# A hybrid decoder layer on one core: filler projections moved ahead of a triangular solve, a last transpose behind a filler, and an output projection begun feature tile by feature tile

## The chip, the cores and the metric

The kernel runs on one core of one Trainium2 chip. The core has a matrix engine (TensorE, PE in the profile), a vector engine (VectorE, DVE), a scalar engine (ScalarE, ACT), a general engine (GpSimd, POOL) and SyncE (SP), which here issues the DMA transfers. Each engine works through its own row of instructions in order, and waits on semaphores for the others. The metric is the device time of one execution in microseconds (us), the median of the runs.

## The reference

One layer on `x` of 1024 positions by 1024 features, all in float32:

```python
h = rmsnorm(x, g_mix)
proj = h @ w_in                                   # 64 tiles of 128 output features and 16 more
y_fox = forgetting_attention(fq, fk, fv, ...)     # 8 heads of 64
y_sc = sb * causal_dwconv(sc * sv, sc_conv_w)
o_dn = gated_delta_rule(l2norm(dq), l2norm(dk_), dv_, g, beta)   # 4 heads of 128
y_dn = rmsnorm(o_dn, dn_norm_gain) * silu(z)
merged = jnp.sum(jnp.einsum('bsnc,ncd->bsnd', ys, w_branch) * gates, axis=2)
x = x + merged @ w_o
...
# gated_delta_rule: for each chunk a unit lower triangular system
a_mat = jnp.where(strict, einsum(kb, kc) * decay, 0.0) + jnp.eye(c)
sol = lax.linalg.triangular_solve(a_mat, rhs, left_side=True, lower=True, unit_diagonal=True)
```

After it come an up projection with a convolution and a gate, a down projection and a per-layer embedding, which the change does not touch.

## The kernel before, in words

Activations lie with the features on the partitions, as eight tiles of 128 features by 1024 positions. Each f32 operand is split in a high and a low part (`split`, L129 on ScalarE, L130 on VectorE or POOL), and one 128 x 128 block of weights is three matmuls of 128x512 (`step`, all at L126): high by high, high by low, low by high. `dense` makes an output tile in two halves of 512 positions; a half of a tile over all eight feature tiles is 24 matmuls into one PSUM bank, and then `evac` reads the bank.

The program is a row of stages. `fx` holds the first norm, the attention, and in `f2` the DeltaNet part; `la`/`me` the gates, the short convolution, the three branch products and the output projection; then come the up and the down stage.

**The DeltaNet stage.** `dn_solve` inverts the triangular systems. For each of eight pairs of chunks ("chunk" below) and four heads it loads kc (tile `kc`, 4 buffers) and a row of decays (`gb`, 3 buffers), multiplies kc by itself on TensorE (tiles `sm`), builds A on VectorE, moves the 32 x 32 diagonal blocks together (L728), and inverts all of them at once by a recursion over 31 rows on VectorE (L734, L736). The inverses are transposed back into TT (L739) and into X (L748), and then products on TensorE put blocks of 64 and of 128 together (`to64`, `add64`, `to128`, `add128`), of which the first is X by A1. `dn_prep` loads ks, qc and vc of a chunk and transposes them on TensorE through one bank (tiles `ev`; L796, L800; VectorE reads them at L797 and L801), `dn_state` carries the state from chunk to chunk (products of w and X, vn, S), and `dn_out` makes a chunk's output in the bank `po`, squares it on ScalarE (L854), scales it (L855 to L859), transposes it (L862) and stores it.

**Fillers.** These stages leave TensorE free in places. So 32 output tiles of the first projection that are needed only later lie in `spare["r"]`: each ("r") is a `raw_tile`, that is a weight load (`wr`, 2 buffers), its split into `wo` (5 buffers), 48 matmuls in two banks, and for each bank an evacuation by ScalarE (L503) and a store (L504). `filler` takes such tiles and gives them to the scheduler with the condition that they come after a matmul noted by `mark`:

```python
def filler(kinds, back=LAG):
    for k in kinds:
        if spare.get(k):
            with tc.issue_after(marks[max(0, len(marks) - 1 - back)]):
```

How many stand where is in the table `PLAN`. The final order on each engine is set by a scheduler that simulates the program, so that table and code order steer it, but don't fix it. In `f2` fillers have two PSUM banks, `sm` four, `ev` and `po` one each.

**The output projection** (L1030 to L1041). `mh` holds the merged activations, eight feature tiles split in two halves each. A feature tile is merged when the third branch (b == 2) has been multiplied by its gate (L1019) and added (L1020, on POOL), and then split at L129 and L130. Then `dense` makes one output tile after another over all eight feature tiles, with six PSUM banks; `ev_o` (L1036) adds x.

Of the kernel before, what the change touches and what calls it, by code (L numbers as in the profile page):

```python
# [10 lines left out]
ALU = mybir.AluOpType  # L11
# [19 lines left out]
PLAN = {"start": "krr", "tail": "rr", "solve": "rrrrrrrrrrrrr",  # L31
        "steps": ["rr", "r", "r", "r", "r", "r", "r", "r", "r"],
# [16 lines left out]
def hybrid_block(ctx: ExitStack, tc: tile.TileContext, I, out, dbg=None):  # L49
# [37 lines left out]
    def bank(role):  # L87
        pool, n = homes[role]
        return pool.tile([P, 512], F32, tag=role, name=nm(role), bufs=n)
# [565 lines left out]
    def hs(h):  # L655
        return slice(h * P, h * P + P)
# [53 lines left out]
    def dn_solve():  # L710
# [26 lines left out]
        for b in range(4):  # L737
            p = slice(32 * b, 32 * b + 32)
            V.transpose(out=TT[p, :, p].rearrange("p x c -> p c x"), in_=TL[p].rearrange("p r c -> p c r"))  # L739
        Ac, Tc = ([x[:, 4 * c : 4 * c + 4, :] for c in range(8)] for x in (A, TT))  # L740
# [105 lines left out]
    def dn_out(c, Sst, vn, pd, qe):  # L846
# [13 lines left out]
        pot = bank("po")  # L860
        for h in range(4):
            nc.tensor.transpose(pot[:, hs(h)], o[:, hs(h)], ident)  # L862
        yo = pt("yo", 2)
        S.activation(yo, pot, AF.Copy, scale=col(C_NG))
        Q.dma_start(ydn[:, :, hs(c)], chunk(yo))
# [15 lines left out]
    with phase("fx", psum=dict(mm=MM, ev=1), cv=3, o=4, sg=2, h=1, l=1, y=1,  # L881
# [31 lines left out]
        with phase("f2", psum=dict(sm=SM2, po=1), X=8, et=2):  # L913
            mark()
            with phase("f2s"):
                Xs = dn_solve()
                mark()
                filler(PLAN["solve"], 1)
            with phase("f2t"):
                preps = [dn_prep(0), dn_prep(1)]  # L920
                Ss, vns = [None], []
                for c in range(9):
# [5 lines left out]
                    if c:  # L928
                        dn_out(c - 1, Ss[c - 1], vns[c - 1], *preps[c - 1][3:])
                    if 2 <= c + 1 < 8:  # L930
                        preps.append(dn_prep(c + 1))
                    filler(PLAN["steps"][c], 1)
                filler("r" * len(spare["r"]), 0)

# [9 lines left out]
    with phase("la", psum=dict(mm=6, sm=2), a=16, wq=3):  # L944
        with phase("me", tmp=9, sg=4, yr=4):
# [50 lines left out]
            for b in range(3):  # L996
# [5 lines left out]
                for d2 in range(4):  # L1002
# [9 lines left out]
                    for dt in (2 * d2, 2 * d2 + 1):  # L1012
                        def ev_b(nb, ps, dt=dt):
# [6 lines left out]
                            G.tensor_tensor(out=m, in0=m, in1=t, op=ALU.add)  # L1020
# [9 lines left out]
            x2s = []  # L1030
            for dt in range(8):
                x2 = big()
                Q.dma_start(x2, I["xT"][dt])

                def ev_o(nb, ps):
                    V.tensor_tensor(out=x2[:, NB[nb]], in0=ps, in1=x2[:, NB[nb]], op=ALU.add)  # L1036
                dense(wload(I["wo"][dt]), KT, mh, ev_o)
                summed = sumsq(acc, x2, dt == 0, (V, G))
                Q.dma_start(x2dr[dt], x2)
                x2s.append(x2)  # L1040
# [216 lines left out]
```

## Time and profile before

| | us |
|---|---|
| median of 3 runs | 2005.56 (2003.4 to 2006.41) |
| the profiled execution | 2005.48 |
| its span, first to last instruction | 2003.7 |
| VectorE / ScalarE / POOL busy in it | 1338.9 / 908.0 / 531.3 |
| chain that ended last, by engine: PE / DVE | 17% / 10% |

The profile is that of one execution. The mean granted TensorE clock is 0.992 of full speed. The chain that ended last is followed back only as far as waits lead, and most of the span TensorE simply works one matmul after another, so the chain names little; where TensorE stands idle, and for whom, is read from its waits. In the names of the rows "mm<-xg,wo" is a matmul of activations xg with weights wo into a bank mm; the buffer's number is left out in the trace and is there in the order of instructions.

### The profile page before, as it was taken

How to read it: one execution, taken by the hardware profiler on the slowest of the kernel's cores; microseconds unless marked ns; L12 is line 12 of the kernel's file. 1: busy time of each engine (PE TensorE's matmuls, PEld its weight loads, DVE VectorE, ACT ScalarE, POOL GpSimd, SP SyncE). 2: the span in 40 equal slices, each digit the busy share in tenths (PEclk: the TensorE clock that was granted, in tenths of full speed). 3: DMA queues.
4: the chain of work that ended last, by engine and by line, in shares of the span. 5: the costliest groups of instructions: out<-in, count | busy, mean ns of one | idle time of the engine just before them, and what ended most of it. 6: DMA issues, size and time to landing. Idle time of an engine off the chain costs nothing. (4 is left out here: it accounts for less than half of the span.)

```text
span 2003.7 us, 25407 instructions
## 1 busy us (share of the span) xinstructions
PE 1943.1 (97%) x9281; PEld 1611.3 (80%) x9281; DVE 1338.9 (67%) x2157; ACT 908.0 (45%) x1651; POOL 531.3 (27%) x435
## 2 busy tenths in 40 slices
PE   8999999999997999999999999999999999999998
PEld 6888888888786888878888787778777778888887
DVE  6878788788496203429757438787878788544564
ACT  6576777677321324333423326454444444211351
POOL 1455334434322222100034110333434340000210
PEclk9999999999998999999999999999999999999999
DMA  4221112122521334447853423112222226332132
GB/s 176 70 98 57 59 59 76 62 83 76 150 91 53 100 106 126 122 155 281 302 191 121 174 91 130 53 47 91 75 84 74 84 74 252 115 95 78 49 114 86
DMA packets 102636, 219.40 MB, mean 109 GB/s; under 512 B 9360, under 2 KB 40432, under 8 KB 102512
## 3 DMA queue, kind: packets, MB, share of 16 engines
q1 hardware_dynamic: 102512, 217.79, 32.1%
q8 instruction: 73, 1.20, 0.3%
q14 instruction: 51, 0.42, 0.1%
HBM read 158.98 MB, written 58.77 MB: 109 GB/s over the span
## 5 line engine op out<-in xcount | busy, mean ns | idle before, releaser
L126 PE MATMUL mm<-xg,wo 128*128 128x512 f32 x6128 | 1488.0, 393 | 17.7 <-DVE wo L130 12.2
L126 PEld LDWEIGHTS mm<-xg,wo 128*128 128x128 f32 x6128 | 1141.7, 189 | 260.6 <-DVE wo L130 19.4
L126 PE MATMUL mm<-a,wo 128*128 128x512 f32 x1216 | 306.1, 391 | 3.1 <-ACT a L129 3.1
L126 PEld LDWEIGHTS mm<-a,wo 128*128 128x128 f32 x1216 | 229.8, 189 | 52.2 <-ACT a L129 4.2
L129 ACT ACTIVATE wo<-wr 128x512 fp32r<-128x512 f32 x232 | 144.6, 626 | 267.8 <-PE mm L126 255.1
L130 POOL TENSOR_TENSOR wo<-wr,wo 128x512 fp32r<-128x512 f32 x108 | 149.1, 1383 | 320.0 <-ACT wo L129 312.1
L1159 DVE TENSOR_TENSOR a<-mm,a 128x512 f32<-128x512 f32 x96 | 65.3, 689 | 92.1 <-PE mm L126 92.0
L130 DVE TENSOR_TENSOR wo<-wr,wo 128x512 fp32r<-128x512 f32 x124 | 89.6, 724 | 27.4 <-ACT wo L129 26.8
L280 POOL TENSOR_TENSOR tmp<-tmp,tmp 128x512 f32<-128x512 f32 x21 | 27.8, 1324 | 286.0 <-ACT tmp L278 284.1
L1020 POOL TENSOR_TENSOR a<-a,sg 128x512 f32<-128x512 f32 x32 | 48.1, 1508 | 191.7 <-DVE sg L1019 191.5
L130 DVE TENSOR_TENSOR wo<-wq,wo 128x512 fp32r<-128x512 f32 x68 | 79.2, 1167 | 3.2 <-ACT wo L129 3.2
L503 ACT ACTIVATE o<-mm 128x512 f32<-128x512 f32 x60 | 35.8, 596 | 93.9 <-PE mm L126 62.5
L1072 DVE SCALAR_TENSOR_TENSOR o<-cw,cols,o 128x1024 f32<-128x1024 f32 x44 | 77.8, 1769 | 0.0
L491 DVE SCALAR_TENSOR_TENSOR o<-cv,cols,o 128x512 f32<-128x512 f32 x72 | 69.9, 971 | 10.2 <-ACT o L489 9.2
L129 ACT ACTIVATE wo<-ws 128x512 fp32r<-128x512 f32 x80 | 50.2, 630 | 56.7 <-PE mm L126 54.9
L600 ACT ACTIVATE pp<-pp,small 128x512 f32<-128x512 f32 (+2 forms) x96 | 58.4, 610 | 28.7 <-DVE small L594 28.4
L1104 POOL TENSOR_TENSOR cg<-o,cg 128x1024 f32<-128x1024 f32 x22 | 55.5, 2522 | 39.7 <-ACT cg L1103 39.7
L199 POOL TENSOR_TENSOR ws<-wq 128x512 f32<-128x512 f32 x20 | 29.7, 1487 | 122.7 <-DMA wq<-wup 122.7
L1070 ACT ACTIVATE o<-cw,cols 128x1024 f32<-128x1024 f32 x22 | 25.4, 1156 | 74.8 <-DVE cw L223 74.8
L130 DVE TENSOR_TENSOR pl<-pq,ph 128x512 fp32r<-128x512 f32 (+1 forms) x80 | 49.9, 629 | 13.9 <-ACT ph L129 13.5
L199 POOL TENSOR_TENSOR ws<-wq,wq 128x512 f32<-128x512 f32 x20 | 43.7, 2183 | 56.3 <-DVE wo L130 52.3
L199 DVE TENSOR_TENSOR ws<-ws,wq 128x512 f32<-128x512 f32 x20 | 14.9, 745 | 64.2 <-POOL ws L199 64.2
(290 smaller groups left out, 2456.7 us busy)
## 6 DMA issues: line engine op xcount, KB each, us to landing
wr<-win SPq DMA_DIRECT2D x64, 512.0 KB, 3.6
wq<-wup SPq DMA_DIRECT2D x44, 512.0 KB, 3.6
r<-o SPq DMA_DIRECT2D x64, 256.0 KB, 2.5
ad<-o SPq DMA_DIRECT2D x20, 512.0 KB, 3.9
wq<-ad SPq DMA_DIRECT2D x20, 512.0 KB, 4.8
wr<-wdn SPq DMA_DIRECT2D x20, 512.0 KB, 3.8
yr<-r SPq DMA_DIRECT2D x16, 512.0 KB, 4.7
sg<-r SPq DMA_DIRECT2D x32, 256.0 KB, 3.3
```

The lines of the kernel that those rows point to most:

```text
L126: pe[0] = nc.tensor.matmul(o, lhsT=l, rhs=r, start=start, stop=stop, skip_group_check=more)
L129: S.activation(h, x, AF.Copy)
L130: (eng or V).tensor_tensor(out=l, in0=x, in1=h.bitcast(F32), op=ALU.subtract)
L199: (G if e == "g" else V).tensor_tensor(out=o, in0=x, in1=y, op=op)
L280: eng[nb].tensor_tensor(out=acc[nb], in0=acc[nb], in1=sq, op=ALU.add)
L491: V.scalar_tensor_tensor(out=o, in0=cv[:, i : i + 512], scalar=col(c0 + i), in1=o, op0=ALU.mult, op1=ALU.add)
L503: S.activation(o, ps, AF.Copy)
L600: S.activation(t[:, :w], t[:, :w], AF.Exp, bias=mn[:, k - 1 : k], scale=-1.0, accum_out=sm[:, i : i + 1])
L1020: G.tensor_tensor(out=m, in0=m, in1=t, op=ALU.add)
L1072: V.scalar_tensor_tensor(out=o, in0=cv[:, i : i + T], scalar=col(c0 + i), in1=o, op0=ALU.mult, op1=ALU.add)
L1104: G.tensor_tensor(out=sg, in0=o, in1=sg, op=ALU.mult)
L1159: V.tensor_tensor(out=x2[dt][:, NB[nb]], in0=ps, in1=x2[dt][:, NB[nb]], op=ALU.add)
```

## The change

Three things are changed. In `PLAN`, of the 13 fillers between solve and chunk steps, one is laid out ahead of the solve ("ahead"), eight inside it between the recursion and the first products ("recursion"), and four stay ("solve"); the steps hold eight in place of ten, and what is left over is laid out behind the last step, as before. In `dn_out` the transposes of the output become a function `turn`, called directly behind `dn_out` except for the last chunk, where it comes after the last matmul of the last filler. In the output projection the first two output tiles are made together, feature tile by feature tile, into four banks, and the merged add of the last feature tiles of the third branch goes from POOL to VectorE.

```diff
-PLAN = {"start": "krr", "tail": "rr", "solve": "rrrrrrrrrrrrr",
-        "steps": ["rr", "r", "r", "r", "r", "r", "r", "r", "r"],
+PLAN = {"start": "krr", "tail": "rr", "ahead": "r", "recursion": "rrrrrrrr", "solve": "rrrr",
+        "steps": ["rr", "r", "r", "r", "r", "r", "r", ""],
...
             V.transpose(out=TT[p, :, p].rearrange("p x c -> p c x"), in_=TL[p].rearrange("p r c -> p c r"))
+        filler(PLAN["recursion"], 0)
...
-        pot = bank("po")
-        for h in range(4):
-            nc.tensor.transpose(pot[:, hs(h)], o[:, hs(h)], ident)
-        yo = pt("yo", 2)
-        S.activation(yo, pot, AF.Copy, scale=col(C_NG))
-        Q.dma_start(ydn[:, :, hs(c)], chunk(yo))
+
+        def turn():
+            pot = bank("po")
...
+        return turn
...
             mark()
+            filler(PLAN["ahead"], 0)
             with phase("f2s"):
...
-                        dn_out(c - 1, Ss[c - 1], vns[c - 1], *preps[c - 1][3:])
-                    if 2 <= c + 1 < 8:
-                        preps.append(dn_prep(c + 1))
-                    filler(PLAN["steps"][c], 1)
+                        turn = dn_out(c - 1, Ss[c - 1], vns[c - 1], *preps[c - 1][3:])
+                    if c < 8:
+                        if c:
+                            turn()
+                        if 2 <= c + 1 < 8:
+                            preps.append(dn_prep(c + 1))
+                        filler(PLAN["steps"][c], 1)
                 filler("r" * len(spare["r"]), 0)
+                with tc.issue_after(pe[0].ins):
+                    turn()
...
-                            G.tensor_tensor(out=m, in0=m, in1=t, op=ALU.add)
+                            (V if b == 2 and dt > 5 else G).tensor_tensor(out=m, in0=m, in1=t, op=ALU.add)
...
-                dense(wload(I["wo"][dt]), KT, mh, ev_o)
-                summed = sumsq(acc, x2, dt == 0, (V, G))
-                Q.dma_start(x2dr[dt], x2)
-                x2s.append(x2)
+                x2s.append(big())
+                Q.dma_start(x2s[dt], I["xT"][dt])
+                if dt == 0:
+                    continue
+                if dt == 1:
+                    ws = [wload(I["wo"][i]) for i in range(2)]
+                    ps = [mmb() for _ in range(4)]
+                    for kt in range(KT):
+                        for i in range(4):
+                            step(ps[i], ws[i // 2], kt, mh[kt], i % 2, kt == 0, kt == KT - 1)
+                    for i in range(4):
+                        ev_o(i % 2, ps[i], x2s[i // 2])
+                else:
+                    dense(wload(I["wo"][dt]), KT, mh, lambda nb, ps, x2=x2s[dt]: ev_o(nb, ps, x2))
+                for i in (0, 1) if dt == 1 else (dt,):
+                    summed = sumsq(acc, x2s[i], i == 0, (V, G))
+                    Q.dma_start(x2dr[i], x2s[i])
```

In the changed kernel the lines are numbered one higher behind L739, three higher from about L860, and ten higher around L950 to L1030 (L1019 is L1029, L1020 is L1030, L950 is L960, L1036 is L1043).

The order of instructions on TensorE around the solve, before: from the last of the eight products of kc with itself (`sm_5892` and `sm_5907` are the first two products of X and A1, `sm_5914` the first of `add64`; `mm_` are fillers).

```order
L126 MATMUL sm_5770<-kc_5768 128x128 x4
L126 MATMUL mm_6278<-xg_245,wo_6275 128x512
...
L126 MATMUL mm_6631<-xg_173,wo_6597 128x512
...
L126 MATMUL sm_5892<-X_5884,A_1231_5890 128x128 x4
L126 MATMUL mm_6631<-xg_232,wo_6600 128x512
...
L126 MATMUL mm_6668<-xg_245,wo_6665 128x512
L126 MATMUL sm_5907<-X_5899,A_1235_5905 128x128 x4
L126 MATMUL sm_5914<-sw_5897,TT_5618 128x128 x4
L126 MATMUL sm_5915<-TT_5618,sw_5897 128x128 x4
```

And now, the same products (`sm_5835`, `sm_6477`, `sm_6492`, `sm_6499`):

```order
L126 MATMUL sm_5835<-kc_5833 128x128 x4
L126 MATMUL mm_5958<-xg_259,wo_5955 128x512
...
L126 MATMUL mm_6441<-xg_271,wo_6410 128x512
L126 MATMUL sm_6477<-X_6469,A_1294_6475 128x128 x4
L126 MATMUL mm_6798<-xg_173,wo_6792 128x512
...
L126 MATMUL mm_6826<-xg_173,wo_6792 128x512
L126 MATMUL sm_6492<-X_6484,A_1298_6490 128x128 x4
L126 MATMUL sm_6499<-sw_6482,TT_5683 128x128 x4
L126 MATMUL sm_6500<-TT_5683,sw_6482 128x128 x4
```

Counted over the whole listing, 326 filler matmuls stand between the start of the DeltaNet stage and the first product before and 432 now; the products of kc stand in two blocks of four behind 48 and 67 of them; 28 and now 25 fillers stand between the first and the second product; and from the last product of the solve to the first transposes of `dn_prep` (`ev` at L796, now L797) there are 189 before and 86 now.

TensorE at the end of the DeltaNet stage, before (`po_8356` the output of chunk 6, `ev_8239`, `ev_8245`, `ev_8252` the transposes of chunk 7's operands and its sums, `sm_8349` its product of w and X, `po_8460` its output, `po_8491` the last transposes, `mm_8530` the first tile of the next stage):

```order
L126 MATMUL po_8356<-S_8009,qe_8062 128x128
L126 MATMUL mm_8404<-xg_173,wo_8398 128x512
...
L796 MATMUL ev_8239<-cst,ks_8229 128x128 x4
...
L126 MATMUL sm_8340<-S_8185,ks_8229 128x128 x4
...
L126 MATMUL mm_8432<-xg_233,wo_8401 128x512
L126 MATMUL ev_8252<-cst,qe_8238 128x1 x4
L126 MATMUL sm_8349<-w_8339,X_6120 128x128 x4
...
L126 MATMUL po_8460<-vn_8354,pd_8237 128x128
L862 MATMUL po_8491<-cst,on_8489 128x128 x4
L126 MATMUL mm_8530<-xg_173,wo_8524 128x512
```

And now (`po_8395` is the output of chunk 7):

```order
L126 MATMUL po_8356<-S_8009,qe_8062 128x128
L797 MATMUL ev_8239<-cst,ks_8229 128x128 x4
...
L126 MATMUL sm_8340<-S_8185,ks_8229 128x128 x4
L801 MATMUL ev_8245<-cst,vc_8231 128x128 x4
L126 MATMUL ev_8252<-cst,qe_8238 128x1 x4
L126 MATMUL sm_8349<-w_8339,X_6705 128x128 x4
L126 MATMUL mm_8435<-xg_173,wo_8429 128x512
...
L126 MATMUL po_8395<-vn_8354,pd_8237 128x128
L126 MATMUL mm_8463<-xg_233,wo_8432 128x512
...
L126 MATMUL mm_8463<-xg_271,wo_8432 128x512
L865 MATMUL po_8491<-cst,on_8424 128x128 x4
L126 MATMUL mm_8530<-xg_173,wo_8524 128x512
```

All fillers that stood between `po_8356` and `sm_8349` have gone behind `sm_8349`, and 11 of them stand between `po_8395` and `po_8491`.

VectorE ahead of the output projection, before (`mm_10137` and `mm_10152` are the two banks of feature tile 6 of the third branch, `mm_10167` and `mm_10182` those of tile 7):

```order
L1019 TENSOR_TENSOR sg_10113<-mm_10137,sg_10113 128x512
L130 TENSOR_TENSOR xg_10228<-a_9170,a_10227 128x512
L950 TENSOR_TENSOR sg_10125<-sg_10125,rs_427 128x512
L1019 TENSOR_TENSOR sg_10117<-mm_10152,sg_10117 128x512
L130 TENSOR_TENSOR xg_10234<-a_9171,a_10233 128x512
```

And now:

```order
L1029 TENSOR_TENSOR sg_10113<-mm_10137,sg_10113 128x512
L130 TENSOR_TENSOR xg_10228<-a_9170,a_10227 128x512
L1030 TENSOR_TENSOR a_9171<-a_9171,sg_10113 128x512
L960 TENSOR_TENSOR sg_10125<-sg_10125,rs_427 128x512
L1029 TENSOR_TENSOR sg_10117<-mm_10152,sg_10117 128x512
L130 TENSOR_TENSOR xg_10234<-a_9171,a_10233 128x512
L1030 TENSOR_TENSOR a_9171<-a_9171,sg_10117 128x512
```

The merged add L1030 now stands on VectorE ahead of the read of `mm_10152`. TensorE's first matmuls of the output projection, now (`a_10197` and `xg_10198` are feature tile 0's two parts, `a_10203` belongs to feature tile 1):

```order
L126 MATMUL mm_10269<-xg_10198,wo_10254 128x512
L126 MATMUL mm_10269<-a_10197,wo_10254 128x512
L126 MATMUL mm_10270<-a_10197,wo_10262 128x512
L126 MATMUL mm_10270<-xg_10198,wo_10262 128x512
L126 MATMUL mm_10270<-a_10197,wo_10262 128x512
L126 MATMUL mm_10271<-a_10197,wo_10262 128x512
L126 MATMUL mm_10271<-xg_10198,wo_10262 128x512
L126 MATMUL mm_10271<-a_10197,wo_10262 128x512
L126 MATMUL mm_10268<-a_10203,wo_10254 128x512
```

Four banks take turns by feature tile, where before one bank (`mm_10258`) took its 24 matmuls in a row.

## Rows read from the trace of the kernel before

**Rows 1.** The page's first section: busy time, share of the span and instructions of each engine.

```profile
PE 1943.1 (97%) x9281; PEld 1611.3 (80%) x9281; DVE 1338.9 (67%) x2157; ACT 908.0 (45%) x1651; POOL 531.3 (27%) x435
```

**Rows 2.** TensorE's waits over the whole span: engine, operation, line, what it waited for, and then us in total, times, longest us.

```profile
PE sm L126 <- DVE X L748: 12.2, 1, 12.2
...
PE sm L126 <- DMA kc<-kdr: 4.0, 4, 2.2
PE po L862 <- DVE yr L959: 3.8, 1, 3.8
PE mm L126 <- ACT a L129: 3.1, 2, 2.5
...
PE mm L126 <- DVE xg L130: 0.9, 1, 0.9
PE po L126 <- DVE pd L813: 0.6, 1, 0.6
```

**Rows 3.** The timeline of TensorE from the fillers beside the recursion to the first product, and from the last product to the first chunk's transposes: start us, us, engine, line, operation, out<-in, count, and in brackets the idle time before it and what ended that.

```profile
559.49 51.84 PE L126 MATMUL mm<-xg,wo 128*128 128x512 f32 x228
623.51 2.07 PE L126 MATMUL sm<-X,A 128*128 128x128 f32 x8 [12.18 <-DVE X L748]
...
681.26 43.15 PE L126 MATMUL mm<-xg,wo 128*128 128x512 f32 x189
724.24 0.60 PE L796 MATMUL ev<-cst,ks 128*128 128x128 f32 x4
```

**Rows 4.** The timeline of VectorE at the end of the recursion (columns as in rows 3).

```profile
611.43 8.78 DVE L739 STREAM_TRANSPOSE TT<-TL 32x1024 f32<-32x1024 f32 x4
620.24 9.06 DVE L748 STREAM_TRANSPOSE X<-TT 32x128 f32<-32x128 f32 x32
```

**Rows 5.** Stretches of the span: from:to us, length, busy us of PE, PEld, DVE, ACT and POOL (with instructions), granted TensorE clock as a share of full speed, DMA share, GB/s.

```profile
614.00:618.00 4.00, 0.00 (x0) 0.00 (x0) 3.97 (x2) 0.00 (x0) 0.00 (x0) 0.50 0.36 125
626.00:628.00 2.00, 2.00 (x8) 1.53 (x7) 1.88 (x7) 0.22 (x1) 0.95 (x1) 0.62 0.00 0
534.00:536.00 2.00, 0.31 (x2) 0.00 (x0) 1.97 (x8) 1.88 (x4) 0.00 (x0) 1.00 0.85 242
886.00:888.00 2.00, 2.00 (x7) 1.61 (x6) 0.00 (x0) 1.55 (x2) 0.00 (x0) 0.50 0.03 8
890.00:892.00 2.00, 2.00 (x9) 1.64 (x8) 0.00 (x0) 0.00 (x0) 0.00 (x0) 0.92 1.03 354
1112.00:1114.00 2.00, 1.12 (x2) 0.40 (x2) 2.00 (x4) 0.11 (x1) 0.65 (x1) 0.55 0.22 33
1116.00:1118.00 2.00, 2.00 (x6) 1.54 (x6) 2.00 (x3) 2.00 (x4) 0.15 (x1) 0.50 1.01 395
```

**Rows 6.** The timeline of TensorE at the first products of kc with itself (columns as in rows 3).

```profile
536.50 1.13 PE L126 MATMUL sm<-kc 128*128 128x128 f32 x8 [2.18 <-DMA kc<-kdr]
```

**Rows 7.** The timeline of ScalarE after the solve (columns as in rows 3): the last exponentials of the decays of the first two chunks, and the evacuation of a filler's bank.

```profile
695.62 0.63 ACT L707 ACTIVATE et<-et 128x512 f32<-128x512 f32 x1 [2.34 <-DVE et L705]
696.16 0.58 ACT L503 ACTIVATE o<-mm 128x512 f32<-128x512 f32 x1
```

**Rows 8.** The timeline of all engines at the end of the DeltaNet stage (columns as in rows 3): TensorE's products and transposes, ScalarE's squares, VectorE.

```profile
861.07 0.38 PE L126 MATMUL po<-S,qe 128*128 128x128 f32 x2
...
864.48 0.39 PE L126 MATMUL po<-vn,pd 128*128 128x128 f32 x2
864.70 1.06 PE L126 MATMUL sm<-S,ks 128*128 128x128 f32 x8
...
866.26 0.39 PE L126 MATMUL po<-vn,pd 128*128 128x128 f32 x2
...
866.69 0.28 ACT L854 ACTIVATE dump<-po 128x128 f32<-128x128 f32 x1 [4.30 <-PE po L126]
...
868.29 0.16 DVE L856 SCALAR_TENSOR_TENSOR small<-small,small 128x4 f32<-128x4 f32 x1 [3.29 <-ACT dump L854]
868.37 0.69 DVE L801 TENSOR_TENSOR bv<-ev,beta 128x512 f32<-128x512 f32 x1
...
869.28 1.12 DVE L825 SCALAR_TENSOR_TENSOR w<-sm,nbe,bv 128x128 f32<-128x128 f32 x4
...
881.14 0.39 PE L126 MATMUL po<-vn,pd 128*128 128x128 f32 x2
885.31 1.09 PE L862 MATMUL po<-cst,on 128*128 128x128 f32 x4 [3.78 <-DVE yr L959]
886.05 26.32 PE L126 MATMUL mm<-xg,wo 128*128 128x512 f32 x106
```

**Rows 9.** The timeline of all engines at the start of the output projection (columns as in rows 3); the last row is of the view of instructions by line: line, engine, operation, out<-in, count, duration in ns as least/median/most, and the start of the first and of the last in us.

```profile
1105.78 0.39 PE L126 MATMUL mm<-a,wo 128*128 128x512 f32 x1
1105.84 0.68 DVE L950 TENSOR_TENSOR sg<-sg,rs 128x512 f32<-128x512 f32 x1
...
1106.44 0.68 DVE L1019 TENSOR_TENSOR sg<-mm,sg 128x512 f32<-128x512 f32 x1
...
1107.27 1.60 POOL L1020 TENSOR_TENSOR a<-a,sg 128x512 f32<-128x512 f32 x1 [3.83 <-DVE sg L1019]
...
1107.64 1.78 DVE L950 TENSOR_TENSOR sg<-sg,rs 128x512 f32<-128x512 f32 x1
...
L1036 DVE TENSOR_TENSOR a<-mm,a x16: 680/692/692, 1120.1 to 1199.8; 128x512 f32<-128x512 f32 x16
```

More of the change, by code (lines that the diff above doesn't have):

```diff
@@ L859, in dn_out @@
         V.tensor_tensor(out=chunk(o), in0=chunk(po), in1=ro.unsqueeze(2).to_broadcast(eb), op=ALU.mult)
-        pot = bank("po")
-        for h in range(4):
-            nc.tensor.transpose(pot[:, hs(h)], o[:, hs(h)], ident)
-        yo = pt("yo", 2)
-        S.activation(yo, pot, AF.Copy, scale=col(C_NG))
-        Q.dma_start(ydn[:, :, hs(c)], chunk(yo))
+        def turn():
+            pot = bank("po")
+            for h in range(4):
+                nc.tensor.transpose(pot[:, hs(h)], o[:, hs(h)], ident)
+            yo = pt("yo", 2)
+            S.activation(yo, pot, AF.Copy, scale=col(C_NG))
+            Q.dma_start(ydn[:, :, hs(c)], chunk(yo))
+        return turn
     spare.update({kd: [lambda kd=kd, h=h: dn_tile(kd, h) for h in range(4)] for kd in "kvq"})
@@ L1030, in hybrid_block, with ev_o @@
             x2s = []
+            def ev_o(nb, ps, x2):
+                V.tensor_tensor(out=x2[:, NB[nb]], in0=ps, in1=x2[:, NB[nb]], op=ALU.add)
             for dt in range(8):
[L1032 to L1036, printed above, removed]
-                dense(wload(I["wo"][dt]), KT, mh, ev_o)
-                summed = sumsq(acc, x2, dt == 0, (V, G))
-                Q.dma_start(x2dr[dt], x2)
-                x2s.append(x2)
+                x2s.append(big())
[15 more added lines that the diff above has]
+                    Q.dma_start(x2dr[i], x2s[i])
             ph = []
```

## The prediction

> **What bounds the kernel now.** I read the page's first section, then TensorE's waits over the whole span, then TensorE and VectorE side by side around the longest waits, and last the granted clock there. TensorE (PE) is busy 1943.1 of 2003.7 us [rows 1]: about 60 us of idle are all that a change of order can win, and beside them what runs at the lower clock. The reader is to see in the list of waits [rows 2] that one wait alone is 12.2 us: the solve's first product waits for VectorE's X (L748). The others that the change can touch are 4.0 (loads of kc before the solve), 3.8 and 0.6 (end of the DeltaNet stage), 3.1 and 0.9 (start of the output projection).
>
> Around the solve, TensorE runs out of fillers at 559.49 + 51.84 = 611.33 and goes on at 623.51 [rows 3]. VectorE runs without a gap all that time: transposes into TT 611.43 to 620.21, then into X [rows 4]. So VectorE is late, and fillers that only lie elsewhere fill the hole. After the last solve product 189 filler matmuls run in a block from 681.26 to 724.24 [rows 3], where little else needs TensorE. That is the stock from which the change takes. One matmul of a filler costs (724.24 − 681.26) / 189 = 0.2274 us. The idle also costs clock: the granted clock is 0.50 (1.2 of 2.4 GHz) from 614 to 618 and 0.62 as a mean of 626 to 628 [rows 5]; if that is half and then full, it turned at 626 + 2 × (1 − 0.62) / 0.5 = 627.5.
>
> **Part A: eight fillers ahead of the solve's first product.** By the order of instructions, 326 filler matmuls stand on TensorE between the stage's start and that product before, 432 now: 106 × 0.2274 = 24.1 us more. After the solve 86 are left of the 189. TensorE then reaches the product at 611.3 + 24.1 = 635.4, less about 3 for the kc waits below and the clock: I take 632 to 635. VectorE is ready for it at 623.5, so it is 8.5 to 12 us early; the wait is gone, and TensorE becomes the late one.
> - Idle removed: 12.2.
> - Clock: 627.5 − 623.51 = 4.0 us of work ran at half, so 2.0 come back if the clock now stays up.
> - kc waits, 4.0 in all [rows 2]: the eight kc·kcᵀ groups now stand in two blocks of four, behind 48 and 19 more fillers, so their loads have longer; on SP's queue, though, a weight load and a store of a filler stand ahead of kc 4 to 7. I take 3 left, a gain of 1.0; bounds −1 (they add as much again as the first 1 us) and +2.2 (the longest single one [rows 6] goes).
> - After the solve the cover is 86 × 0.2274 = 19.6 us in place of 43. Under it lie the loads of the first two chunks and their decay factors. In the profile the last of these on ScalarE is done at 696.25, 15.0 after 681.26, and the evacuation of a filler's bank (L503) stands directly behind it [rows 7]. In the new order that evacuation frees the bank which the filler 62 matmuls after the solve needs, 62 × 0.2274 = 14.1 after it. So about 0.7 of wait comes; bounds 0 and 1.5.
> Sum of A: 12.2 + 2.0 + 1.0 − 0.7 = 14.5; with the bounds, 11 to 16.5.
>
> The steps inside the solve keep their spacing (25 filler matmuls in place of 28 before the second product), so they cost nothing more. The fillers' own splits stand ahead of the first A1 product (L751) on POOL; that step has the 8.5 us of slack to be late in.
>
> **Part B: last transposes behind a filler.** TensorE ends chunk 7's products at 881.14 + 0.39, and its last transposes start at 885.31 after 3.78 idle; the clock falls to 0.50 in 886 to 888 and is back at 0.92 as a mean of 890 to 892 [rows 5, 8]; 890 + 2 × 0.08 / 0.5 puts its return at 890.3. Now 11 filler matmuls, 2.5 us, stand between. The chain from the products through ScalarE's squares and VectorE's scaling to the transposes takes 885.31 − 881.14 = 4.17, so 4.17 − 2.5 and a little issue leave 1.5. These fillers come from further up, and that makes a new wait: TensorE's order now has ev_8239, ev_8245, ev_8252 and the product sm_8349 without a filler between. They share one ev bank. ev_8252 needs VectorE's read of ev_8245 (L801), and that stands on VectorE behind L856, which waits for the squares (dump, L854) of the chunk before. In the profile the last product of po_8356 starts at 866.26 and ends at 866.65, L856 comes 1.6 later, L801 directly behind it, and L825, for which sm_8349 waits, from 869.28 to 870.40 [rows 8]. Moved up: the first product starts at 861.07 as before, ev_8239 takes 0.4, the other seven products 0.22 each (864.70 − 864.48 [rows 8]), so they end at 863.2, L856 comes at 864.9, L801 is done about 865.7 and ev_8252 starts at 865.85. TensorE has only sm_8340 (1.06, some 0.9 to the next start) and ev_8245 (0.35 by my estimate) before it and is there at 864.45: 1.4 of wait, and 0.3 more before sm_8349, since L825 follows L801. Idle 3.8 + 0.6 = 4.4 becomes 1.5 + 1.4 + 0.3 = 3.2: gain 1.2, and 0.4 as the transposes take 1.09 at half clock. If the clock stays up, (890.3 − 886.05) / 2 = 2.1 more, with 886.05 from the filler behind the transposes [rows 8]. Sum of B 3.7; bounds 0 (idle only moved, clock falls all the same) and 5 (the new waits are nothing).
>
> **Part C: the first two output tiles by feature tile.** Before, the first tile wants all eight feature tiles within 24 matmuls while VectorE, POOL and ScalarE still make them: waits of 3.1 + 0.9 = 4.0 [rows 2], and a clock of 0.55 as a mean of 1112 to 1114 and 0.50 in 1116 to 1118 [rows 5]. The 16 halves are 384 matmuls, 87.3 us at 0.2274; from 1105.78 [rows 9] they could end at 1193.1. The last evacuation (L1036) starts at 1199.8 [rows 9], some 0.15 after its last matmul, so 6.5 are lost. Now each feature tile feeds 12 matmuls, 2.7 us, so feature tile k is due 2.7 k after the start, and the last two at 1105.78 + 18.9 at the earliest, long after they are made. What comes instead is a wait for banks. Four are wanted at once, and the fourth (mm_10271, due 1107.83) is that of mm_10152, which VectorE frees with its read of feature tile 6, the last L1029 but two. VectorE's row of work from 1106.44: L1029 0.68, a split 0.68, the merged add L1030 0.68 (moved over from POOL, where it takes 1.60 [rows 9]; price of L1029, same shape), L960 0.68, L1029 again: about 1109.7, a wait of 1.9. Gain 6.5 − 1.9 = 4.6; bounds 3 and 6.
>
> In the profile L950 (now L960) takes 1.78 beside POOL's L1020 and 0.68 alone [rows 9]. By the Trainium skill ("GPSIMD Engine Reference", § 8 Key points) POOL shares its SBUF interfaces with VectorE, which contends above all in instructions with two SBUF inputs; the trace agrees, 1.78 against 0.68. Since the add leaves POOL, I take 0.68; were L960 still at 1.78 beside other POOL work, the wait would be 3.0 and C 3.5.
>
> **Sum.** 14.5 + 3.7 + 4.6 = 22.8 off the profiled execution's 2005.48 (span 2003.7 and 1.8 around it), 0.1 below the median of the runs: 1982.7. The later stages keep their order and their waits.
>
> **Rivals.**
> - The clock falls in the new short waits. The 1.4 + 0.3 and 1.5 in the tail and the 1.9 in the output projection could each take it down for some microseconds. For: waits of 0.6 (3.1 less its longest, 2.5) and 0.9 [rows 2] went before a mean of 0.55 in 1112 to 1114. Against: the wait of 2.18 that ended at 536.50 left it at 1.00 [rows 5, 6]. Price: B loses its 2.1, C about 2.0: 1986.8. The Trainium skill ("TensorE: Matmul & The Clock Gate", section "A second HAM failure mode: psum-queue depth-cycling") says that frequent small idles between groups of matmuls can make the clock swing; the two rows speak for it and against it. Chance 0.13.
> - The tail's idle is only moved: the new wait chain is as long as the old one, B gives 0. For: L801 behind L856. Against: the chain is shown step by step. 1986.4. Chance 0.12.
> - The cover after the solve is too thin. Slower: 19.6 us of filler must hide loads, decay and bank reads for two chunks; each microsecond beyond is idle on TensorE. It decides against the change when that chain takes 19.6 + 22.8 = 42.4 us, as much as the whole block of before; then about 2006. Against: its last step came 15.0 after the solve. A mean stretch (25 to 30 us) gives 1988 to 1993. Chance 0.04 for slower, 0.06 for the middle.
> - The change does not do what it says, since VectorE or POOL delays X with the fillers' splits by more than 8.5 us: A gives back what is beyond. POOL makes those splits, not VectorE, whose row up to X has no gap to fill [rows 4], so little: with the whole of A given back, 1997; 0.02.
> - kc waits vanish and no bank wait comes: A 17.5, 1979.7; 0.08.
>
> My forecast has the remaining 0.55, its own range 1980 to 1986. The range of 8 in 10 takes in the third rival's milder half: 1978 to 1991. A measurement of this kernel tells 0.2%, 4 us, from no change: faster 0.93, the same 0.03, slower 0.04.
>
> **What would show it.** Of after: no wait for X of more than 1 us before the first product, granted clock 1.00 through 612 to 628, VectorE waiting for TensorE at L764; after the solve at most a microsecond or two for an evacuation; in the tail about 3 us in three waits and no 0.50 behind; in the output projection one wait of 2 to 3 us for a bank and none for a feature tile. It is wrong if a new wait of over 5 us stands before the first chunk's transposes, or if the product still waits for X.

## The result and the profile after

The changed kernel takes 1984.5 us (1980.78 to 1987.8, 4 runs), the kernel before 2005.46 in the same sitting; the ratio is 0.9896 (95% interval 0.9877 to 0.9916), that is 20.9 us less by the medians, where 22.8 were forecast. The spans of the two profiled executions, 2003.7 and 1981.7, differ by 22.0. Cut at the starts of the same instructions, that difference lies here (us, each from the timeline of TensorE; the first row counts 24.1 of filler moved into it, the second 24.1 moved out; the output projection is taken to the start of its last matmul):

| stretch | before | after | gain |
|---|---|---|---|
| first filler of the DeltaNet stage to first product of X | 101.84 | 111.10 | 24.1 − 9.26 = 14.8 |
| to the first chunk's transposes | 100.73 | 74.74 | 25.99 − 24.1 = 1.9 |
| to the last transposes | 161.07 | 160.63 | 0.4 |
| to the output projection (the gates stage) | 220.47 | 220.61 | −0.1 |
| the output projection | 93.6 | 88.8 | 4.8 |
| the rest | | | 0.2 |

TensorE's waits in the changed kernel (columns as in rows 2):

```profile
PE mm L126 <- DVE wo L130: 12.3, 17, 3.0
...
PE sm L126 <- DMA kc<-kdr: 1.9, 2, 1.3
...
PE mm L126 <- DVE sg L1029: 1.4, 1, 1.4
PE mm L126 <- DVE a L1026: 1.3, 2, 0.7
...
PE po L865 <- ACT wo L129: 1.2, 1, 1.2
PE ev L126 <- DVE bv L802: 1.1, 1, 1.1
...
PE sm L126 <- DVE A L722: 0.4, 1, 0.4
```

The 12.2 for X of [rows 2] is gone, and so are the 3.8 at the last transposes and the 3.1 of the output projection. New are 1.4 for a bank (L1029), 1.1 for bv, 1.2 at the last transposes (the row names a split of weights on ScalarE, but what the transposes read is scaled by VectorE, at L860, from 867.43 to 868.12, just ahead of them), and 1.3 for L1026, which no step of the prediction had. Around the solve, TensorE first and then VectorE, against [rows 3, 4]:

```profile
632.90 1.05 PE L126 MATMUL sm<-X,A 128*128 128x128 f32 x8
...
687.98 19.82 PE L126 MATMUL mm<-xg,wo 128*128 128x512 f32 x86
707.64 0.60 PE L797 MATMUL ev<-cst,ks 128*128 128x128 f32 x4
```

```profile
624.13 9.07 DVE L749 STREAM_TRANSPOSE X<-TT 32x128 f32<-32x128 f32 x32
641.48 0.69 DVE L765 TENSOR_TENSOR X<-X,sm 128x512 f32<-128x512 f32 x1 [8.28 <-PE sm L126]
```

No idle time stands before the product, and VectorE, late before, now waits 8.28 for TensorE. Behind the solve ScalarE does its last exponential and then the evacuation, as in [rows 7], 13.5 us after 687.98:

```profile
700.91 0.63 ACT L707 ACTIVATE et<-et 128x512 f32<-128x512 f32 x1 [2.60 <-DVE et L705]
701.45 0.58 ACT L503 ACTIVATE o<-mm 128x512 f32<-128x512 f32 x1
```

It ends at 702.03, just before the bank is wanted (687.98 + 14.1 = 702.1), and no wait came. The tail, TensorE, and the granted clock behind the first of its two waits (columns as in rows 5):

```profile
847.58 0.60 PE L801 MATMUL ev<-cst,vc 128*128 128x128 f32 x4
849.30 1.05 PE L126 MATMUL ev<-cst,qe 128*128 128x1 f32 x8 [1.13 <-DVE bv L802]
...
864.25 2.77 PE L126 MATMUL mm<-xg,wo 128*128 128x512 f32 x11
868.27 0.63 PE L865 MATMUL po<-cst,on 128*128 128x128 f32 x4 [1.25 <-ACT wo L129]
```

```profile
850.00:852.00 2.00, 2.00 (x13) 2.00 (x13) 1.36 (x6) 0.63 (x1) 0.84 (x1) 0.62 0.00 0
852.00:854.00 2.00, 2.00 (x7) 1.53 (x6) 0.00 (x0) 0.60 (x1) 0.43 (x1) 0.52 0.00 0
```

After the wait of 1.13 the clock was at half for some 3.4 us, which costs 2 × 0.38 + 2 × 0.48 = 1.7; after that of 1.25 it stayed up (1.00 in 870 to 872). The gates stage has three short waits that [rows 2] did not have:

```profile
965.51 7.37 PE L126 MATMUL mm<-xg,wo 128*128 128x512 f32 x31 [0.21 <-DVE xg L130]
973.62 11.20 PE L126 MATMUL mm<-xg,wo 128*128 128x512 f32 x48 [0.74 <-DVE a L1026]
985.39 103.65 PE L126 MATMUL mm<-xg,wo 128*128 128x512 f32 x456 [0.57 <-DVE a L1026]
```

And the start of the output projection, all engines, against [rows 9]:

```profile
1090.80 0.69 DVE L1030 TENSOR_TENSOR a<-a,sg 128x512 f32<-128x512 f32 x1
...
1091.40 0.68 DVE L960 TENSOR_TENSOR sg<-sg,rs 128x512 f32<-128x512 f32 x1
...
1092.01 0.68 DVE L1029 TENSOR_TENSOR sg<-mm,sg 128x512 f32<-128x512 f32 x1
...
1092.74 0.50 PE L126 MATMUL mm<-a,wo 128*128 128x512 f32 x1 [1.38 <-DVE sg L1029]
```

One wait for the fourth bank, behind the add (L1030) and L960 on VectorE, and no wait for a feature tile.

### The profile page after: what moved, and what is told of

Same layout as the page of the kernel before. It is cut to its first block, busy times and chain, and to the rows that moved or that the text cites. A ratio compares the mean times of both kernels' runs of the same rounds, so it can differ in the third digit from the quotient of the medians.

```text
span 1981.7 us, 25403 instructions
## 1 busy us (share of the span) xinstructions
PE 1938.0 (98%) x9281; PEld 1608.2 (81%) x9281; DVE 1337.2 (67%) x2161; ACT 907.7 (46%) x1651; POOL 526.8 (27%) x431
## 5 line engine op out<-in xcount | busy, mean ns | idle before, releaser
L1030 POOL TENSOR_TENSOR a<-a,sg 128x512 f32<-128x512 f32 x28 | 42.4, 1520 | 191.9 <-DVE sg L1029 191.9
L130 DVE TENSOR_TENSOR pl<-pq,ph 128x512 fp32r<-128x512 f32 (+1 forms) x80 | 49.9, 628 | 13.9 <-ACT ph L129 13.5
```

The lines of the kernel that those rows point to most:

```text
L130: (eng or V).tensor_tensor(out=l, in0=x, in1=h.bitcast(F32), op=ALU.subtract)
L1030: (V if b == 2 and dt > 5 else G).tensor_tensor(out=m, in0=m, in1=t, op=ALU.add)
```

## The experiments

Executions of one kernel spread here over up to 8 us, so beside the times (medians, ratio to the kernel before with its interval) the stretches of each profile are given, as in the table above; they are gathered at the end of this section.

**e1: the table of fillers alone.** The kernel before with the two calls of `filler` and

```diff
+PLAN = {"start": "krr", "tail": "rr", "ahead": "r", "recursion": "rrrrrrrr", "solve": "rrrr",
+        "steps": ["rr", "r", "r", "r", "r", "r", "r", "", ""],
```

> The kernel before with the new PLAN and the two new filler calls alone; dn_out and the output projection as before. Theory 1 (the table of fillers does all that changed in the DeltaNet stage, its tail included, and the output projection adds its own part): the wait for X is gone, the first chunk's transposes come 16.6 us earlier than before, the tail has the waits of the changed kernel (1.1 for bv, 1.2 at the last transposes) and not the 3.8, the output projection loses 6.5 us as before; time 1984.5 + 4.8 = 1989, give or take 2. Rival (the parts are as the prediction cut them, the tail belongs to turn): the 3.8 at the last transposes stays; 2005.5 - 14.5 = 1991.

1987.25 us, ratio 0.9917 (0.9903 to 0.9931). Its waits:

```profile
PE sm L126 <- DMA kc<-kdr: 3.0, 1, 3.0
...
PE po L863 <- ACT wo L129: 1.2, 1, 1.2
PE ev L126 <- DVE bv L802: 1.1, 1, 1.1
```

Theory 1 holds: with `dn_out` as before, the 3.8 at the last transposes is gone all the same and the tail has the changed kernel's two waits. The table alone moves the last filler behind chunk 7's product (it is laid out with `back` 0 in place of 1), and with it the tail's order. One part of the expectation is missed: the first chunk's transposes start at 711.67, 12.6 us earlier than before and not 16.6, since TensorE waited 3.0 for kc and the clock was at half from there to about 553.

**e12: turn undone.** The changed kernel, with

```diff
-                        if c:
-                            turn()
...
-                with tc.issue_after(pe[0].ins):
-                    turn()
```

and `turn()` called directly behind `dn_out` for every chunk. Its order of instructions is that of the changed kernel: in the two traces all rows of TensorE, ScalarE, POOL and SyncE follow in the same order, and on VectorE all but one MEMSET of two columns, which stands one place later.

> The changed kernel with the transposes of dn_out called where they were before; the scheduler gives the same order of instructions on every engine. Theory 1 (turn changes nothing, and what differs between two executions is where the clock falls after a short wait): the changed kernel again, 1981 to 1988, its profile with the same waits, and the clock at half in other places. Rival (turn matters beyond the order): the 3.8 at the last transposes is back, 1987.

1984.71 us, ratio 0.9898 (0.9884 to 0.9913): the changed kernel again. Its profile is a second execution of the same program. Here the first stretch shows a loss that the first execution did not have, and the tail, with the same wait of 1.1 for bv (ended at 851.47), kept its clock:

```profile
546.00:548.00 2.00, 0.88 (x4) 0.92 (x5) 0.00 (x0) 0.00 (x0) 0.00 (x0) 0.74 0.76 225
548.00:550.00 2.00, 2.00 (x11) 2.00 (x11) 0.00 (x0) 0.00 (x0) 0.00 (x0) 0.50 0.47 138
...
852.00:854.00 2.00, 2.00 (x16) 1.91 (x16) 1.53 (x7) 1.07 (x2) 0.68 (x1) 1.00 0.00 0
```

So `turn` does nothing, and where the clock falls differs between two executions of one program.

**e2: the output projection alone.** The kernel before with that part of the diff from `merged` to the last store of x2.

> The kernel before with the change of the output projection alone (four banks by feature tile, the last merged adds on VectorE). Theory 1 (its gain is its own): one wait for a bank of 1 to 3 us, granted clock 1.00 behind it, 6.5 lost becomes 2; time 2005.5 - 4.8 = 2000.7. Rival (in the changed kernel it gained because the stage ahead left the engines in other places): waits of over 3 us or the clock at half for some microseconds; time 2003 to 2005.

1999.06 us (12 runs), ratio 0.9971 (0.9961 to 0.998), 5.8 less.

```profile
PE sm L126 <- DVE X L748: 12.2, 1, 12.2
...
PE mm L126 <- DVE sg L1019: 1.0, 1, 1.0
```

Theory 1 holds: the stretch takes 88.1 in place of 93.6, with one bank wait of 1.0. The gains of e1 and e2, 0.83% and 0.29%, make 1.12%, and the change has 1.04 (0.84 to 1.23): the parts add up.

**e4: merged adds on POOL.** The changed kernel with

```diff
-                            (V if b == 2 and dt > 5 else G).tensor_tensor(out=m, in0=m, in1=t, op=ALU.add)
+                            G.tensor_tensor(out=m, in0=m, in1=t, op=ALU.add)
```

> The changed kernel with all merged adds on POOL again. Theory 1 (the order by feature tile alone removes the waits; the move of four adds to VectorE only sets how long the fourth bank is waited for): bank wait between 0.7 (no add in VectorE's row) and 2.5 (L960 slow beside POOL, 1.78 against 0.68), nothing else; time 1984.5 +- 1. Rival (the adds on POOL make the last feature tiles late, as before): waits for feature tiles 6 and 7 of 2 us or more, clock down; 1987 to 1989.

1983.06 us, ratio 0.9898 (0.9884 to 0.9912). The timeline of all engines there:

```profile
1088.88 1.59 POOL L1030 TENSOR_TENSOR a<-a,sg 128x512 f32<-128x512 f32 x1 [3.64 <-DVE sg L1029]
...
1089.25 1.77 DVE L960 TENSOR_TENSOR sg<-sg,rs 128x512 f32<-128x512 f32 x1
...
1091.67 0.50 PE L126 MATMUL mm<-a,wo 128*128 128x512 f32 x1 [1.86 <-DVE sg L1029]
```

Theory 1 holds. L960 takes 1.77 beside POOL's add and 0.68 when the add is VectorE's own; yet the bank comes only 0.5 later, since the add left VectorE's row. The order by feature tile does the work, the move of the adds is worth half a microsecond.

**e3: the old tail.** The changed kernel with

```diff
-                filler("r" * len(spare["r"]), 0)
+                filler("r" * len(spare["r"]), 1)
```

> The changed kernel with the last filler allowed one mark earlier, which gives the tail the order that it had before (10 fillers ahead of ev_8239, none ahead of the last transposes). Theory 1 (what the tail gains, 0.8 us up to the next stage and 2.1 of clock behind it, is lost again in the gates stage, where VectorE's reads of the branch banks come late): the 3.8 wait and the half clock return, the waits for L1026 of the gates stage (1.3 in all) go; time within 1 us of the changed kernel, 1984 to 1985.5. Rival (the tail's gain reaches the end): 2.9 slower, 1987.4.

1984.75 us, ratio 0.9907 (0.9891 to 0.9922). The 3.8 is back, L1026 is not waited for:

```profile
PE po L865 <- DVE yr L969: 3.8, 1, 3.8
PE sm L126 <- DMA kc<-kdr: 3.6, 1, 3.6
```

The median lies where theory 1 has it, but the interval covers the rival too. By the profiles, tail and gates stage together take 161.06 + 221.21 = 382.3 here, 381.5 before and 381.2 in the changed kernel, but 378.3, 379.8, 379.2, 381.6 and 379.7 in e1, e4, e8, e9 and e12, which have its tail. The waits for L1026 are gone, and yet the gates stage is no shorter, since the clock was at half at its start (0.66 in 874 to 876, 0.50 in 876 to 878). So the new tail is worth between nothing and 4 us, by the execution; the runs do not tell it closer. What this profile lost more was ahead of the solve. Its rows of TensorE, and the clock behind:

```profile
548.23 6.45 PE L126 MATMUL sm<-kc 128*128 128x128 f32 x32 [3.59 <-DMA kc<-kdr]
```

```profile
548.00:550.00 2.00, 1.77 (x8) 1.80 (x9) 0.00 (x0) 0.00 (x0) 0.00 (x0) 0.50 0.35 91
```

The kernel before kept its clock behind its longest wait of this kind, 2.18 [rows 6]:

```profile
536.00:538.00 2.00, 1.14 (x9) 1.01 (x9) 1.04 (x3) 0.27 (x1) 1.65 (x2) 1.00 0.67 186
```

**e5: the last filler in three pieces.** The changed kernel with

```diff
-                filler("r" * len(spare["r"]), 0)
+                u = spare["r"].pop(0)
+                last = pe[0].ins
+                with tc.issue_after(marks[-2]):
+                    w, kts, mov, evac = raw_tile(u)
...
+                for at, js in ((marks[-1], range(4)), (last, range(4, kts))):
+                    with tc.issue_after(at):
+                        for j in js:
+                            step(ps, w, j, mov[j], 1, j == 0, j == kts - 1)
```

> The changed kernel with the last filler laid out in three pieces: its first bank may come one mark earlier (the order then has 10, 5 and 9 of its matmuls from po_8356 to ev_8252), half of its second bank stays behind sm_8349, and the other half, 12 matmuls, comes after chunk 7's output and ahead of the last transposes. Theory 1 (the gates stage loses again what the tail gains): the 1.1 for bv goes, about 1.3 stays at the last transposes, the clock stays at 1.00 in the tail, and the start of the output projection comes no earlier, since the gates stage waits 1.5 to 3 us for VectorE; time 1984 to 1985. Rival (the tail's gain reaches the end): 1.1 of wait and up to 1.7 of half clock less, 1982 to 1983.

1980.0 us, ratio 0.9881 (0.9865 to 0.9897). No wait for bv; the tail's waits are

```profile
PE po L865 <- DVE on L860: 1.1, 1, 1.1
...
PE po L126 <- ACT yo L867: 0.9, 1, 0.9
```

with the clock at 1.00 in 850 to 852 and 866 to 870. The gates stage took 219.7, less than in the changed kernel, so nothing is seen of theory 1's loss there. The median lies below the rival's 1982 to 1983 too, and how much of it is the spread's is not shown: tail and gates stage take 378.4 here, and e1, with the filler in one piece, took 378.3. What the profiles show is the tail alone: spread, it took 158.7 to 158.8 in all three (e5, e7, e10), with no half clock; in one piece 159.0 to 159.1 in the five where the clock stayed up (e1, e4, e6, e8, e12), and 160.6 and 160.7 where it fell (changed kernel, e9).

**e6 and e7: splits on POOL**, without and with the tail of e5:

```diff
-                    split(h, l, y)
+                    split(h, l, y, G if b == 1 else None)
```

> The changed kernel with the low parts of the second branch's four operands (xg from yr, L130) made on POOL, which does nothing in that stretch, so that on VectorE no split that waits for a load stands ahead of the reads of the first branch's banks (L1026). Theory 1 (those reads are late because VectorE stands at such a split): TensorE's waits for L1026, 1.3 in all, go to under 0.3, the stretch from the last transposes to the output projection, 220.6 us in the changed kernel, becomes 218.5 to 219.3; time 1983. Rival (VectorE or the loads as a whole are late there): the waits stay or move to another line of VectorE, the stretch stays above 220; time 1984.5.

1986.03 us, ratio 0.9909 (0.9894 to 0.9923). Three engines in the stretch where L1026 is waited for:

```profile
974.83 10.51 POOL L130 TENSOR_TENSOR xg<-yr,xg 128x1024 fp32r<-128x1024 f32 x4 [119.29 <-ACT xg L129]
```

```profile
977.78 2.50 DVE L130 TENSOR_TENSOR wo<-wr,wo 128x512 fp32r<-128x512 f32 x1 [3.88 <-ACT wo L129]
...
980.80 5.10 DVE L130 TENSOR_TENSOR wo<-wr,wo 128x512 fp32r<-128x512 f32 x2
```

```profile
988.36 5.99 PE L126 MATMUL mm<-xg,wo 128*128 128x512 f32 x18 [2.09 <-DVE a L1026]
```

Theory 1 falls as a remedy: beside POOL's splits VectorE's splits of weights take 2.3 to 2.9 us each, which in the changed kernel take 0.68; L1026 stands behind them, the wait grows to 2.1, and the stage to 223.7. The Trainium skill ("GPSIMD Engine Reference", § 8 Key points) has POOL share its SBUF interfaces with VectorE, with contention in instructions of two SBUF inputs; these splits have two, and the trace agrees, 2.5 against 0.68. The traces show more than that. In the kernel before, 62 of VectorE's 128x512 TENSOR_TENSORs that read no PSUM begin while one of POOL's is running; 56 of them end 0.55 us after POOL's, whenever they began, and take up to 2.5, where alone they take 0.69 (the other six keep about 0.7; why is open). The 74 that read one input from PSUM, as L1026 does, take 0.67 to 0.69. So what such an instruction loses goes by how long POOL's still has to run: POOL's splits of 128x1024 run 2.4 to 2.8 here, its merged add in e4 1.6. That VectorE stood at a split when it should have read the bank is seen in the trace of the changed kernel, but was not shown to be what costs.

> Both edits of the two runs before. If each gain is its own: no wait for bv, none for L1026, the clock at 1.00 through the tail; the stretch from the first chunk's transposes to the output projection, 381.2 in the changed kernel, comes to 377 to 378; time 1980.5 to 1981.5. Rival (the gates stage has another limit behind VectorE, its loads): 380 to 381 and 1984.

1984.2 us, ratio 0.9898 (0.9882 to 0.9914); tail and gates 158.7 + 221.8 = 380.5, with 1.8 of wait for the read of a bank (L1040 there): the rival's numbers. By the profiles the splits on POOL cost the gates stage 2.1 against e5.

**e8 and e11: how many fillers the recursion can take.** The changed kernel with

```diff
-"recursion": "rrrrrrrr", "solve": "rrrr"
+"recursion": "rrrrrrrrr", "solve": "rrr"
```

and in e11 with twelve and none.

> The changed kernel with nine fillers in the recursion and three behind the solve. 38 filler matmuls, 8.6 us, are left between the last solve product and the first chunk's transposes, where the changed kernel has 86. Theory 1 (the cover behind the solve is used up to about 14 us: the evacuation behind the last exponential of the decays): a new wait of about 14 - 8.6 = 5 us behind the solve, the clock at half for some microseconds; X is waited for neither way; time 1984.5 + 5 to 8 = 1990 to 1993. Rival (the evacuation can be done in another order and the transposes need only their loads): no wait or under 2 us, 1984 to 1986.

1980.56 us, ratio 0.9884 (0.9866 to 0.9902). TensorE behind the solve, and ScalarE's evacuation:

```profile
698.23 8.92 PE L126 MATMUL mm<-xg,wo 128*128 128x512 f32 x38
706.99 0.60 PE L797 MATMUL ev<-cst,ks 128*128 128x128 f32 x4
```

```profile
711.05 0.58 ACT L503 ACTIVATE o<-mm 128x512 f32<-128x512 f32 x1
```

No wait: theory 1 falls (the median lies below the rival's 1984 to 1986 as well). The transposes need ks alone, and the decays, done 12.9 us behind the solve, are covered by the fillers that stand behind the transposes too (38 + 23 = 61, 13.9 us).

> The changed kernel with all twelve fillers in the recursion and none behind the solve; the solve's inner products then stand without fillers between them. Theory 1 (fillers behind the solve are free to take, those between the solve's products are not: there each product waits for ScalarE's copies and VectorE's subtractions): new waits inside the solve, 8 chunks with some 1 to 2 us each, 8 to 16 us, and the clock at half for much of it; 1995 to 2005. Rival (TensorE's own products cover each other): under 4 us of waits, 1984 to 1988.

1983.41 us, ratio 0.9896 (0.9881 to 0.9911). Between 640 and 760 TensorE waits once:

```profile
PE sm L126 <- POOL A L752: 1.4, 1, 1.4
```

Theory 1 falls again: the solve's bare products cover each other. The cover behind the solve was not nothing, though: the trace has 28 fillers there, 6.7 us, which were laid out for the steps. Eight, nine and twelve fillers give the same time, within what the runs tell.

**e9 and e10: six buffers for kc**, in the changed kernel and with the tail of e5:

```diff
-            kc = pt("kc", 4)
+            kc = pt("kc", 6)
```

> The changed kernel with six buffers for kc in place of four. In five profiles of kernels with the new table the products of kc waited 1.4 to 3.8 us for their loads, and in four of these the granted clock then fell to 0.50 for 4 to 7 us, so that the first product of X and A1 began anywhere between 632.5 and 637.3. Theory 1 (the later four loads stand on SP's queue until the first four buffers are read): waits for kc of 1.5 or less, the first product by 632.5, no clock loss there; the median 1 to 2 us under the changed kernel, 1983. Rival (the loads themselves are late: they land long after their issue, whatever the buffers): waits of 2 to 4 as before; 1984.5.

(The second sentence counts wrongly: eight profiles had been taken with the new table, and in four of the eight the clock fell, for 3.4 to 6.8 us.) 1983.49 us, ratio 0.9888 (0.9868 to 0.9908). TensorE's one wait for kc, and the clock behind it:

```profile
547.48 2.02 PE L126 MATMUL sm<-kc 128*128 128x128 f32 x16 [1.46 <-DMA kc<-kdr]
```

```profile
548.00:550.00 2.00, 2.00 (x17) 1.90 (x16) 0.92 (x4) 0.00 (x0) 0.00 (x0) 1.00 0.50 138
850.00:852.00 2.00, 2.00 (x10) 1.95 (x10) 1.05 (x5) 0.77 (x2) 1.17 (x1) 0.51 0.00 0
```

The stretch does what theory 1 says: the first product at 631.6, the earliest of all profiles with the new table. The median is that of theory 1 and, within the interval, that of the rival; the clock fell in the tail instead. That the buffers are the cause is not shown. In the changed kernel SP waited for a buffer of kc (L717) only 1.5 us, in e8, with four buffers as well, not at all, and the loads took about as long from issue to landing with four as with six (changed kernel, then e9):

```profile
SPq L717 <- PE sm L126: 1.5, 2, 1.0
...
DMA to landing us min/median/max: 6.5/7.6/8.0
...
DMA to landing us min/median/max: 6.4/7.0/8.1
```

> The spread tail of e5 and the six kc buffers together, as the best of what the runs point to. If both hold: 1979 to 1981 and a ratio to the kernel before of 0.987 to 0.988; if the buffers do nothing, as e5: 1980 to 1982.

1979.67 us (1979.22 to 1981.61), ratio 0.988 (0.9864 to 0.9897), beside e12's 0.9898 in the same sitting. It is some 4 us under the eight runs of the changed order (mean of the runs of the changed kernel and e12: 1984.2), though the two intervals overlap; e5 (1980.0) and e8 (1980.56) lie as low, within the noise. The waits for kc were 2.2 in all, in four pieces of at most 0.9, and the clock stayed up.

The stretches of the profiles, in us (e8's first product has 48 more fillers, 10.9 us, ahead of it; e11's fillers stand elsewhere altogether, so it is left out):

| kernel | first product of X | clock ahead of it | last transposes after the first chunk's | gates stage | output projection |
|---|---|---|---|---|---|
| changed | 632.9 | full | 160.6 | 220.6 | 88.8 |
| e12, same order | 635.1 | half | 159.1 | 220.7 | 89.3 |
| e4 | 632.6 | full | 159.1 | 220.7 | 89.5 |
| e1 | 636.4 | half | 159.0 | 219.3 | 93.2 |
| e3 | 637.3 | half | 161.1 | 221.2 | 89.0 |
| e5 | 634.8 | half | 158.7 | 219.7 | 88.5 |
| e6 | 635.8 | half | 159.1 | 223.7 | 88.7 |
| e7 | 632.5 | full | 158.7 | 221.8 | 88.4 |
| e8 | 643.2 | full | 159.1 | 220.1 | 88.3 |
| e9 | 631.6 | full | 160.7 | 220.9 | 88.4 |
| e10 | 632.1 | full | 158.8 | 220.0 | 87.9 |

## Why the prediction came out right

The time and its sign came from part A, as forecast, and its mechanism was right; part B's was not, and the total hides it. Term by term:

- **The idle of 12.2 and the clock of 2.0.** Right. No wait is left before the product, and the solve's own stretch, which ran partly at half clock, is 1.9 shorter.
- **kc, +1.0 within −1 and +2.2.** In this profile 4.0 became 1.9 + 0.4 for A, 1.7 better. But the term was mis-sized: the single longer waits of the new order (2.2 to 3.6 us in e12, e5, e1, e6 and e3) brought the clock to half for some microseconds behind them, which those of the old order (the longest 2.18 [rows 6]) did not, and the first product then began 2 to 5 us later; in e11, with 2.3, and e4, with 2.5, the clock stayed up. The bound of −1 left that out.
- **A bank wait of 0.7 behind the solve.** It did not come; the evacuation was 0.1 early. The 0.7 does not follow from its own rows either: there the evacuation ends at 696.16 + 0.58 = 696.74, 15.5 after the solve, which against 14.1 gives 1.4; in the new order that chain took 14.05. Sum of A by the table 14.8 + 1.9 = 16.7, against 14.5; 0.9 of it has no row among the waits.
- **The cover behind the solve**, on which the slower rival rested, was counted wrongly: as the fillers up to the first transposes. e8, with 38 of them left, shows that those behind the transposes hide the loads and decays as well.
- **Part B, 3.7.** The waits were about right (1.13 for 1.4, 1.25 for 1.5; the 0.3 before the product of w and X did not come), but 0.3 came of it in this profile. Two terms failed. The clock's 2.1 behind the tail came, but 1.7 went at the wait for bv: the first rival, in the tail alone. And the gates stage, of which the sum said that it keeps its waits, waited 1.5 for VectorE. With the two, 3.7 and the 0.8 less of waits leave 1.3; the other 1.0 has no row. Four other profiles with this tail (e1, e4, e8, e12) gained 1.8 to 3.2, e9 nothing. The edit that the change names for it was not the cause either: `turn` changes no instruction's place (e12), the tail's order comes from the table (e1).
- **Part C, 4.6.** 4.8, with the bank wait 1.4 for 1.9 and L960 at 0.68 as taken; e4 measured the other end, 1.77.

Between the two profiles the total was 0.8 short (22.0 for 22.8): A's surplus of 2.2 met B's deficit of 3.4, and C and the rest added 0.4. That it came so close is partly luck. Of the signs that the prediction named, one failed: a clock of 0.50 did stand in the tail. By the medians it was 1.9 short, less than the changed kernel's own runs spread. Of the rivals' prices one is added up wrongly: with no wait for kc and none for the bank A would be 14.5 + 3.0 + 0.7 = 18.2, not 17.5.

## What to carry to other kernels

A hole on the bounding engine is worth its length and the clock lost behind it, whatever the fillers are taken from, as long as their old place has other work (here it had: no wait came behind the solve with 86 or 38 fillers in place of 189); count the work beyond the next step too before calling a cover thin. Where a table and a code edit come together, build each alone and compare the orders: the edit that names the effect may do nothing. Before work goes to an idle POOL, look how long VectorE's instructions beside POOL's take. Price a new wait of a microsecond or two on TensorE with the clock that may go with it, and judge variants that differ by 2 us from several executions, stretch by stretch.

## What was not expected

The clock behind one and the same wait differs between executions: the wait of 1.1 for bv stands in the changed kernel, e1, e4, e6, e8, e9, e11 and e12, and the clock fell behind it in the changed kernel, in e9 and in e11 (0.62, 0.51 and 0.54 as the first mean of 2 us), not in the other five. Why it falls in one execution and not in the next stays open. The kc waits of the same program (changed kernel, e12) were 1.9 and 2.8 in all, and only behind the second did it fall. And VectorE's split of 0.68 us grew to 2.3 to 2.9 beside POOL's, more than the 1.77 that the merged add brought L960 to: in both cases VectorE's instruction ended 0.55 after POOL's.
